# A sliding-window copy with two DMA queues: other staging groups, ten staged batches instead of eleven, 16 KB direct packets

## The chip, the cores and the metric

The kernel runs on one core of a Trainium2 chip. The metric is the device time of one execution in microseconds (us). No compute engine takes part: everything is done by the core's 16 DMA engines, fed by two queues, the direct one (issued by the SyncE engine, SP; q1 in the profile) and the staging one (issued by ScalarE, ACT; q10).

Runs went to several chips of one kind. The kernel before took 757 us on the first and 750 to 752 us on the others, so I compare kernels by their ratio to the kernel before on the same chip. A ratio is the mean time of one kernel's fast runs over that of the other's of the same rounds; it is not quite the ratio of the medians that I quote.

## The reference

```python
batch, length, dim = (32, 4096, 256)      # float32, window_size 64, stride 32
n_windows = (length - window_size) // stride + 1          # 127
for i in range(n_windows):
    start = i * stride
    result[:, i] = x[:, start:start + window_size].copy()
```

In blocks of 32 rows (32 KB) a batch is 128 blocks, and window w is blocks w and w+1. Nearly every block is written twice, as the second (odd) half of one window and the first (even) half of the next.

## The kernel before

A batch is copied in one of two ways. **Direct**: HBM to HBM, each window read as 64 KB; one batch moves 8.3 MB through the DMA engines, and HBM both reads and writes it, 16.6 MB. **Staged**: its 4.2 MB are loaded once into an SBUF tile of 128 partitions and stored twice, as even and as odd halves; 12.6 MB through the engines, 12.6 MB in HBM. Staging so trades engine time for HBM traffic. Eleven batches are staged.

```python
DIRECT, IN, OUT = 32768, 16384, 16384      # largest packets, bytes
# ... class Copier: windows(), load(), store() issue one DMA each
class Staging:                              # 4 tiles of 128 x 32 KB
    def run(self, q):
        bufs = len(self.tiles)
        for g in range(min(bufs, len(self.batches))):
            self.load(q, g)                 # one DMA of 4 MB
        for g in range(len(self.batches)):
            self.store(q, g)                # two DMAs: even halves, odd halves
            if g >= 1 and g - 1 + bufs < len(self.batches):
                self.load(q, g - 1 + bufs)
# ... in the kernel:
staged = [*range(1, B - 3, 3), B - 2]       # 11 batches
spilled = staged[:-1]   # these store all 128 rows; the two rows too many land in
                        # neighbours' windows and are overwritten later by rest()
# ... direct batches, in transfers of 16 windows:
for j in range(7):
    if j % 3 == 1 or (j == 3 and i % 5 != 2):
        c.windows(ring_d, b, w0 + 16 * j, 16, 0)     # split into halves: two transfers
        c.windows(ring_d, b, w0 + 16 * j, 16, 1)
    else:
        c.windows(ring_d, b, w0 + 16 * j, 16)
# ... rest(b): 15 windows, after the neighbours' stores have landed
```

Of the kernel before, what the change touches and what calls it, by code (L numbers as in the profile page):

```python
# [1 line left out]

# [4 lines left out]


DIRECT, IN, OUT = 32768, 16384, 16384


class Copier:


    def __init__(self, nc, tc, x, out, B, L, D, W, S, n_win):
        assert W == 2 * S and L % S == 0
        self.nc, self.tc, self.x, self.out = nc, tc, x, out
        self.B = B
        self.blk = S * D
        self.nb = L // S  # L20
        self.nw = n_win
        self.total = 0
        self.done = tc.alloc_semaphore("done")

    def xap(self, block, dims):
        return bass.AP(self.x.tensor, self.x.offset + block * self.blk, dims)

    def oap(self, elem, dims):
        return bass.AP(self.out.tensor, self.out.offset + elem, dims)

    def count(self, dma):
        dma.then_inc(self.done, 16)
        self.total += 16

    def windows(self, q, b, w0, n, half=None):

        blk = self.blk
        size = 2 * blk if half is None else blk
        off = blk if half else 0
        self.count(  # L40
            q.dma_start(
                out=self.oap((b * self.nw + w0) * 2 * blk + off, [[2 * blk, n], [1, size]]),
                in_=bass.AP(
                    self.x.tensor,
                    self.x.offset + (b * self.nb + w0) * blk + off,
                    [[blk, n], [1, size]],
                ),
                max_dma_last_dim=DIRECT,
            )
        )  # L50

    def load(self, q, t, b):
        return q.dma_start(
            out=t[:, :], in_=self.xap(b * self.nb, [[self.blk, self.nb], [1, self.blk]]),
            max_dma_last_dim=IN,
        )

    def store(self, q, t, b, half, p0=0, n=None):



        blk = self.blk
        n = self.nb if n is None else n
        w = b * self.nw + p0 - half
        return q.dma_start(
            out=self.oap(w * 2 * blk + half * blk, [[2 * blk, n], [1, blk]]),
            in_=t[p0 : p0 + n, :],
            max_dma_last_dim=OUT,
        )


class Staging:


    def __init__(self, c, pool, dtype, batches, bufs):
        self.c, self.batches = c, batches
        self.tiles = [pool.tile([128, c.blk], dtype, name=f"xb{i}") for i in range(bufs)]
        self.loaded = [c.tc.alloc_semaphore(f"loaded{i}") for i in range(bufs)]
        self.stored = [c.tc.alloc_semaphore(f"stored{i}") for i in range(bufs)]

    def load(self, q, g):
        n, i = divmod(g, len(self.tiles))
        if n:
            q.wait_ge(self.stored[i], 32 * n)
        self.c.load(q, self.tiles[i], self.batches[g]).then_inc(self.loaded[i], 16)

    def store(self, q, g):
        n, i = divmod(g, len(self.tiles))
        q.wait_ge(self.loaded[i], 16 * (n + 1))
        if g == len(self.batches) - 1:  # L90

            for half, p0, rows in ((0, 0, 112), (0, 112, 15), (1, 1, 15), (1, 16, 112)):
                self.c.count(self.c.store(q, self.tiles[i], self.batches[g], half, p0, rows))
            return
        for half in (0, 1):
            self.c.store(q, self.tiles[i], self.batches[g], half).then_inc(self.stored[i], 16)

    def wait_stored(self, q, g):
        n, i = divmod(g, len(self.tiles))
        q.wait_ge(self.stored[i], 32 * (n + 1))  # L100

    def run(self, q):
        bufs = len(self.tiles)
        for g in range(min(bufs, len(self.batches))):
            self.load(q, g)
        for g in range(len(self.batches)):
            self.store(q, g)

            if g >= 1 and g - 1 + bufs < len(self.batches):
                self.load(q, g - 1 + bufs)  # L110


@with_exitstack
def kernel(
    ctx: ExitStack,
    tc: tile.TileContext,
    x: bass.AP,
    window_size: bass.AP,
    stride: bass.AP,
    out: bass.AP,  # L120
):
    nc = tc.nc
    W, S = int(window_size), int(stride)
    B, L, D = x.shape
    n_win = (L - W) // S + 1
    assert out.shape == (B, n_win, W, D)
    c = Copier(nc, tc, x, out, B, L, D, W, S, n_win)
    staged = [*range(1, B - 3, 3), B - 2]
    direct = [b for b in range(B) if b not in staged]
    pool = ctx.enter_context(tc.tile_pool(name="xb", bufs=1))  # L130
    st = Staging(c, pool, x.dtype, staged, 4)
    ring_d, ring_s = nc.sync, nc.scalar
    spilled = staged[:-1]

    def rest(b):

        for n in (b - 1, b + 1):
            if n in spilled:
                st.wait_stored(ring_d, spilled.index(n))
        c.windows(ring_d, b, 0 if b - 1 in spilled else 112, 15)  # L140

    with tc.tile_critical():
        st.run(ring_s)



        free = [b for b in direct if b - 1 not in spilled and b + 1 not in spilled]
        direct = free + [b for b in direct if b not in free]
        late = 4
        for i, b in enumerate(direct):  # L150
            w0 = 15 if b - 1 in spilled else 0
            for j in range(7):
                if j % 3 == 1 or (j == 3 and i % 5 != 2):
                    c.windows(ring_d, b, w0 + 16 * j, 16, 0)
                    c.windows(ring_d, b, w0 + 16 * j, 16, 1)
                else:
                    c.windows(ring_d, b, w0 + 16 * j, 16)
            if b in free:
                rest(b)
            elif i >= len(free) + late:  # L160
                rest(direct[i - late])
        for b in direct[-late:]:
            rest(b)
        ring_d.wait_ge(c.done, c.total)


# [1 line left out]
_INS = ['x', 'window_size', 'stride']  # L168
_OUTS = [((32, 127, 64, 256), 'float32')]

_NUMBERS = {'window_size': 64, 'stride': 32}


# [26 lines left out]
```

## Time and profile before

| | kernel before |
|---|---|
| time | 756.73 us median, 4 runs |
| bytes through the DMA engines | 313.2 MB |
| HBM read + written | 220.9 + 267.0 = 487.9 MB |

The page of the kernel before, its parts on time slices and queues. The DMA line gives the busy tenths of the 16 engines in 40 slices of 19 us, the GB/s line what they moved; a queue's line gives packets, MB, and the time its packets took as a share of 16 engines' span.

```profile
DMA  9999999999999999999999999999999999999996
GB/s 372 429 400 423 409 431 426 420 420 408 408 435 418 408 413 430 408 413 434 431 403 418 425 411 408 425 426 402 416 422 428 393 428 423 419 425 422 415 398 294
DMA packets 17949, 313.16 MB, mean 414 GB/s; under 512 B 4169, under 2 KB 4169, under 8 KB 4169
...
q1 hardware_dynamic: 8945, 174.80, 55.2%
q10 hardware_dynamic: 9002, 138.35, 44.1%
...
HBM read 220.92 MB, written 266.99 MB: 644 GB/s over the span
```

The engines are always busy, yet between the first slice and the last the rate swings between 393 and 435 GB/s. A packet that waits for HBM counts as busy. The records of single packets show it. Undisturbed, a 16 KB packet takes 611 ns, a 32 KB packet 1213 ns and a semaphore write 9 ns, each overlapping the next by 3 to 4 ns; longer times are time lost. I call the sum of such excess, averaged over the 16 engines, the *contention*: 22.9 us here.

The DMA view of two stretches of the same run, chosen from the packet records, first one in which the staging queue only stores (204 to 222 us), then one at the change from stores to loads (240 to 252 us). A queue's line has packets, MB and share as above:

```profile
q1 hardware_dynamic: 222, 4.16, 53.8%
q10 hardware_dynamic: 223, 3.59, 46.5%
```

```profile
q1 hardware_dynamic: 138, 2.72, 57.5%
q10 hardware_dynamic: 137, 1.98, 41.0%
```

Two readings. The queues take turns packet by packet (222 against 223, 138 against 137), as the Trainium skill's page "DMA: Bandwidth & Descriptors" (Queues, rings and completion order) says; semaphore writes count as turns. And direct bytes weigh twice in HBM: the first stretch, 18 us long, drew (2 x 4.16 + 3.59) MB / 18 us = 662 GB/s and moved 431 GB/s, no packet lengthened to speak of; the second, 12 us long, drew 618 GB/s and moved 392, its packets 8% over their undisturbed times. Two more stretches of stores (undisturbed) and one more change (8%) look the same.

SP's own waits (total us, times, longest):

```profile
SPq L41 <- DMA out_dram<-xb: 100.2, 6, 42.7
```

These cost nothing as long as the direct queue still holds work, which the slices of the whole page show: they stay at 9 tenths.

### The profile page before, as it was taken

What the parts mean: (1) busy time and instruction counts of PE and PEld (TensorE: products, weight loads), DVE (VectorE), ACT (ScalarE), POOL (GpSimd) and SP (SyncE); (2) the same over time, 40 slices, a digit from 0 to 9 for tenths busy, and PEclk for the clock granted to TensorE, in tenths of its full rate; (3) what the DMA queues carried; (4) which work ended last, traced back from release to release, by engine and by line L of the source; (5) the groups of instructions that cost most, each with busy time, mean ns of one, the idle gap of its engine ahead of it and who ended that gap; (6) DMA issues with size and microseconds to landing.
All of it is one profiled execution on the core that took longest, in us unless ns stands there. A gap on an engine that the chain in (4) does not pass through costs nothing. (4 is left out here: it accounts for less than half of the span.)

```text
span 757.3 us, 312 instructions
## 1 busy us (share of the span) xinstructions
POOL 0.2 (0%) x4
## 2 busy tenths in 40 slices
POOL 0000000000000000000000000000000000000000
DMA  9999999999999999999999999999999999999996
GB/s 372 429 400 423 409 431 426 420 420 408 408 435 418 408 413 430 408 413 434 431 403 418 425 411 408 425 426 402 416 422 428 393 428 423 419 425 422 415 398 294
DMA packets 17949, 313.16 MB, mean 414 GB/s; under 512 B 4169, under 2 KB 4169, under 8 KB 4169
## 3 DMA queue, kind: packets, MB, share of 16 engines
q1 hardware_dynamic: 8945, 174.80, 55.2%
q10 hardware_dynamic: 9002, 138.35, 44.1%
q14 instruction: 2, 0.02, 0.0%
HBM read 220.92 MB, written 266.99 MB: 644 GB/s over the span
## 5 line engine op out<-in xcount | busy, mean ns | idle before, releaser
L181 POOL MEMSET const-bfloat16-1.0<- 128x1 bf16 x1 | 0.1, 102 | 0.0
L181 POOL MEMSET const-uint8-127<- 128x1 uint8 x1 | 0.1, 102 | 0.0
L181 POOL MEMSET const-float32-0.0<- 128x1 f32 x1 | 0.1, 99 | 0.2 <-issue 0.2
L181 POOL MEMSET const-float32-1.0<- 128x1 f32 x1 | 0.1, 99 | 0.0
## 6 DMA issues: line engine op xcount, KB each, us to landing
out_dram<-in_x_dram SPq DMA_DIRECT2D x88, 1024.0 KB, 95.2
out_dram<-xb ACTq DMA_DIRECT2D x20, 4096.0 KB, 115.1
out_dram<-in_x_dram SPq DMA_DIRECT2D x118, 512.0 KB, 94.4
xb<-in_x_dram ACTq DMA_DIRECT2D x11, 4096.0 KB, 90.0
out_dram<-in_x_dram SPq DMA_DIRECT2D x21, 960.0 KB, 95.0
out_dram<-xb ACTq DMA_DIRECT2D x2, 3584.0 KB, 93.4
out_dram<-xb ACTq DMA_DIRECT2D x2, 480.0 KB, 94.9
```

The costliest lines, as they stand in the source:

```text
L181: nc = _bacc.Bacc("TRN2", target_bir_lowering=False, num_devices=1)
```

## The change

It simplifies the kernel. Staging works in groups of 16 blocks, one for each DMA engine, in slots whose 16 partitions lie on 16 different SBUF ports; loads and stores alternate finely, one load and then two stores, with loads ten groups ahead. Ten batches are staged. Direct batches go out as one transfer of 112 windows in 16 KB packets and one of 15 windows in 32 KB packets. No store spills, so SP waits for none. The partitions follow the port map of the skill's page "SBUF — State Buffer" (Door 1: The DMA port swizzle). The diff is shortened; `# ...` marks what is left out.

```diff
-DIRECT, IN, OUT = 32768, 16384, 16384
+DIRECT, STAGE = 16384, 16384
+N_STAGED = 10
+N_TILES = 6
+LEAD = 10
+# class Direct
+        full = self.g.nw // 16 * 16
+        for b in self.batches:
+            self.windows(q, b, 0, full, DIRECT)
+            self.windows(q, b, full, self.g.nw - full, 2 * DIRECT)
+# class Staged
+        self.slots = [t[32 + c : 96 : 4, :] for t in tiles for c in range(4)]
+        self.groups = [(b, j) for b in batches for j in range(0, g.nb, 16)]
+    # ... load(): one DMA of 16 blocks into a slot
+    # ... store(): two DMAs, even and odd halves; 15 rows at a batch's edges
+    def run(self, q, lead):
+        for r in range(lead):
+            self.load(q, r)
+        for r in range(len(self.groups)):
+            if r + lead < len(self.groups):
+                self.load(q, r + lead)
+            self.store(q, r)
-    staged = [*range(1, B - 3, 3), B - 2]
-    # ... rest(), the split window transfers, 4 tiles of 128 partitions
+    staged = Staged(g, tc, pool, x.dtype, range(B - N_STAGED, B), N_TILES)
+    direct = Direct(g, range(B - N_STAGED))
```

More of the change, by code (lines that the diff above doesn't have):

```diff
@@ L6, with __init__, xap, oap @@
 from concourse._compat import with_exitstack
-DIRECT, IN, OUT = 32768, 16384, 16384
-class Copier:
-    def __init__(self, nc, tc, x, out, B, L, D, W, S, n_win):
-        assert W == 2 * S and L % S == 0
-        self.nc, self.tc, self.x, self.out = nc, tc, x, out
-        self.B = B
-        self.blk = S * D
-        self.nb = L // S
-        self.nw = n_win
-        self.total = 0
-        self.done = tc.alloc_semaphore("done")
-    def xap(self, block, dims):
-        return bass.AP(self.x.tensor, self.x.offset + block * self.blk, dims)
-    def oap(self, elem, dims):
-        return bass.AP(self.out.tensor, self.out.offset + elem, dims)
+DIRECT, STAGE = 16384, 16384
+N_STAGED = 10
+N_TILES = 6
+LEAD = 10
+class Geometry:
+    def __init__(self, tc, x, out, B, L, D, W, S, n_win):
+        assert W == 2 * S and L % S == 0 and n_win == L // S - 1
+        self.x, self.out = x, out
+        self.blk, self.nb, self.nw = S * D, L // S, n_win
+        self.done, self.total = tc.alloc_semaphore("done"), 0
+    def xap(self, b, block, dims):
+        return bass.AP(self.x.tensor, self.x.offset + (b * self.nb + block) * self.blk, dims)
+    def oap(self, b, w, half, dims):
+        at = ((b * self.nw + w) * 2 + half) * self.blk
+        return bass.AP(self.out.tensor, self.out.offset + at, dims)
     def count(self, dma):
@@ L33, in count @@
         self.total += 16
-    def windows(self, q, b, w0, n, half=None):
-        blk = self.blk
-        size = 2 * blk if half is None else blk
-        off = blk if half else 0
-        self.count(
-            q.dma_start(
-                out=self.oap((b * self.nw + w0) * 2 * blk + off, [[2 * blk, n], [1, size]]),
-                in_=bass.AP(
-                    self.x.tensor,
-                    self.x.offset + (b * self.nb + w0) * blk + off,
-                    [[blk, n], [1, size]],
-                ),
-                max_dma_last_dim=DIRECT,
-            )
-        )
@@ L52, in load @@
-    def load(self, q, t, b):
-        return q.dma_start(
-            out=t[:, :], in_=self.xap(b * self.nb, [[self.blk, self.nb], [1, self.blk]]),
-            max_dma_last_dim=IN,
-        )
-    def store(self, q, t, b, half, p0=0, n=None):
-        blk = self.blk
-        n = self.nb if n is None else n
-        w = b * self.nw + p0 - half
-        return q.dma_start(
-            out=self.oap(w * 2 * blk + half * blk, [[2 * blk, n], [1, blk]]),
-            in_=t[p0 : p0 + n, :],
-            max_dma_last_dim=OUT,
-        )
@@ L72, with __init__, windows, run @@
-class Staging:
-    def __init__(self, c, pool, dtype, batches, bufs):
-        self.c, self.batches = c, batches
-        self.tiles = [pool.tile([128, c.blk], dtype, name=f"xb{i}") for i in range(bufs)]
-        self.loaded = [c.tc.alloc_semaphore(f"loaded{i}") for i in range(bufs)]
-        self.stored = [c.tc.alloc_semaphore(f"stored{i}") for i in range(bufs)]
-    def load(self, q, g):
-        n, i = divmod(g, len(self.tiles))
+class Direct:
+    def __init__(self, g, batches):
+        self.g, self.batches = g, batches
+    def windows(self, q, b, w0, n, size):
+        g = self.g
+        g.count(
+            q.dma_start(
+                out=g.oap(b, w0, 0, [[2 * g.blk, n], [1, 2 * g.blk]]),
+                in_=g.xap(b, w0, [[g.blk, n], [1, 2 * g.blk]]),
+                max_dma_last_dim=size,
+            )
+        )
+    def run(self, q):
+        full = self.g.nw // 16 * 16
+        for b in self.batches:
+            self.windows(q, b, 0, full, DIRECT)
+            self.windows(q, b, full, self.g.nw - full, 2 * DIRECT)
@@ new lines, with __init__, load @@
+class Staged:
+    def __init__(self, g, tc, pool, dtype, batches, n_tiles):
+        self.g = g
+        tiles = [pool.tile([128, g.blk], dtype, name=f"xb{i}") for i in range(n_tiles)]
+        self.slots = [t[32 + c : 96 : 4, :] for t in tiles for c in range(4)]
+        self.loaded = [tc.alloc_semaphore(f"loaded{i}") for i in range(len(self.slots))]
+        self.stored = [tc.alloc_semaphore(f"stored{i}") for i in range(len(self.slots))]
+        self.groups = [(b, j) for b in batches for j in range(0, g.nb, 16)]
+    def load(self, q, r):
+        g, (b, j) = self.g, self.groups[r]
+        n, i = divmod(r, len(self.slots))
@@ L83, in load, with store @@
         if n:
             q.wait_ge(self.stored[i], 32 * n)
-        self.c.load(q, self.tiles[i], self.batches[g]).then_inc(self.loaded[i], 16)
-    def store(self, q, g):
-        n, i = divmod(g, len(self.tiles))
+        q.dma_start(
+            out=self.slots[i], in_=g.xap(b, j, [[g.blk, 16], [1, g.blk]]),
+            max_dma_last_dim=STAGE,
+        ).then_inc(self.loaded[i], 16)
+    def store(self, q, r):
+        g, (b, j) = self.g, self.groups[r]
+        n, i = divmod(r, len(self.slots))
@@ L89, in store @@
         q.wait_ge(self.loaded[i], 16 * (n + 1))
-        if g == len(self.batches) - 1:
-            for half, p0, rows in ((0, 0, 112), (0, 112, 15), (1, 1, 15), (1, 16, 112)):
-                self.c.count(self.c.store(q, self.tiles[i], self.batches[g], half, p0, rows))
-            return
         for half in (0, 1):
-            self.c.store(q, self.tiles[i], self.batches[g], half).then_inc(self.stored[i], 16)
-    def wait_stored(self, q, g):
-        n, i = divmod(g, len(self.tiles))
-        q.wait_ge(self.stored[i], 32 * (n + 1))
@@ L102, in run @@
-    def run(self, q):
-        bufs = len(self.tiles)
-        for g in range(min(bufs, len(self.batches))):
-            self.load(q, g)
-        for g in range(len(self.batches)):
-            self.store(q, g)
-            if g >= 1 and g - 1 + bufs < len(self.batches):
-                self.load(q, g - 1 + bufs)
+            lo = 1 if half and j == 0 else 0
+            hi = 15 if not half and j + 16 == g.nb else 16
+            dma = q.dma_start(
+                out=g.oap(b, j + lo - half, half, [[2 * g.blk, hi - lo], [1, g.blk]]),
+                in_=self.slots[i][lo:hi, :],
+                max_dma_last_dim=STAGE,
+            )
@@ L113 @@
+            if r + len(self.slots) < len(self.groups):
+                dma.then_inc(self.stored[i], 16)
+            else:
+                g.count(dma)
+    def run(self, q, lead):
[5 more added lines that the diff above has]
+            self.store(q, r)
 @with_exitstack
@@ L126 @@
     assert out.shape == (B, n_win, W, D)
-    c = Copier(nc, tc, x, out, B, L, D, W, S, n_win)
-    staged = [*range(1, B - 3, 3), B - 2]
-    direct = [b for b in range(B) if b not in staged]
+    g = Geometry(tc, x, out, B, L, D, W, S, n_win)
     pool = ctx.enter_context(tc.tile_pool(name="xb", bufs=1))
-    st = Staging(c, pool, x.dtype, staged, 4)
-    ring_d, ring_s = nc.sync, nc.scalar
-    spilled = staged[:-1]
-    def rest(b):
-        for n in (b - 1, b + 1):
-            if n in spilled:
-                st.wait_stored(ring_d, spilled.index(n))
-        c.windows(ring_d, b, 0 if b - 1 in spilled else 112, 15)
-    with tc.tile_critical():
-        st.run(ring_s)
-        free = [b for b in direct if b - 1 not in spilled and b + 1 not in spilled]
-        direct = free + [b for b in direct if b not in free]
-        late = 4
-        for i, b in enumerate(direct):
-            w0 = 15 if b - 1 in spilled else 0
-            for j in range(7):
-                if j % 3 == 1 or (j == 3 and i % 5 != 2):
-                    c.windows(ring_d, b, w0 + 16 * j, 16, 0)
-                    c.windows(ring_d, b, w0 + 16 * j, 16, 1)
-                else:
-                    c.windows(ring_d, b, w0 + 16 * j, 16)
-            if b in free:
-                rest(b)
-            elif i >= len(free) + late:
-                rest(direct[i - late])
-        for b in direct[-late:]:
-            rest(b)
-        ring_d.wait_ge(c.done, c.total)
+    staged = Staged(g, tc, pool, x.dtype, range(B - N_STAGED, B), N_TILES)
+    direct = Direct(g, range(B - N_STAGED))
+    with tc.tile_critical():
+        staged.run(nc.scalar, LEAD)
+        direct.run(nc.sync)
+        nc.sync.wait_ge(g.done, g.total)
 _INS = ['x', 'window_size', 'stride']
```

## The prediction

> **What bounds it.** The page's second part shows the 16 DMA engines busy in every slice but the last (9 tenths; mean 414 GB/s); no compute engine works. The engines are the limit. The trace's packet records show how: on one engine, packets of the two queues alternate strictly, one from each, and follow each other without a gap. A 32 KB packet takes 1213 ns undisturbed, a 16 KB one 611 ns, a semaphore write 9 ns, each overlapping the next by 3 to 4 ns; so a packet costs about 5 ns plus its bytes at 27.2 GB/s. The Trainium skill's page "DMA: Bandwidth & Descriptors" (Queues, rings and completion order) says that an engine takes turns between its queues packet by packet; this trace agrees, semaphore writes counting as turns.
>
> Sum for one of the 15 fuller engines, before: direct 21 x 8 windows x 2 packets x 1209.5 = 406.4 us; staged 11 x 24 blocks x 2 packets x 607.5 = 320.8; semaphores 1.5; together 728.7. Start and end take 3.6. The span is 757.3, so about 25 us (3.4%) are packets that took longer than their undisturbed time. Mean packets say the same: 1248 and 632 ns. I take this for contention in HBM (644 GB/s over the span, page part 3). It is uneven: nearly none while the staged queue stores even halves, about 40 ns lost per us while it loads, bursts of over 100 ns per us at changes from one to the other.
>
> **What the change does.**
> - One direct batch more, one staged fewer, no spilled stores: 313.2 MB moved falls to 308.3 MB. HBM traffic rises from 487.9 to 491.4 MB.
> - Direct packets become 16 KB (windows 112 to 126 stay 32 KB), 5 ns each.
> - Per fuller engine: direct 22 x (28 x 607.5 + 2 x 1209.5) = 427.4 us; staged 10 x 24 x 2 x 607.5 = 291.6; semaphores 1.6; together 720.6. That is 8 us less, all on the critical path.
> - Turns per engine are about 704 (direct) against 720 (staged), so both queues end together as before.
> - The 15-row transfers should leave one engine with about 10% less, as before (the same page's rule: the largest count up to 16 that divides the rows).
> - Waits: the loads run ten groups ahead and 24 slots exist, so the staged queue should never run dry; 240 staging issues at about 0.4 us (ACT's DMA issues, timeline) are hidden. Waits of SP for stores (100 us, SP's waits) vanish, but they cost nothing: the queue was full.
> - Loads and stores are mixed finely at all times, instead of in 4 MB runs. Neighbouring engines now touch neighbouring blocks. This changes the contention, whose sign I cannot read from the trace: the weighted mean of its load and store stretches gives 25 ns per us (18 us), the mixed stretches over 60 (45 us); HBM would have to give 2% more per us.
>
> **Prediction.** 720.6 + 3.6 + about 22 us of contention = 746 us, range 733 to 768. Faster by over 2%: 0.33; within 2%: 0.58; slower by over 2%: 0.09.
>
> **What would show each step.** Moved bytes 308 MB, HBM reads 225 MB and writes 266 MB; undisturbed packets still 611 and 1213 ns; DMA 9 tenths to the last slice; the two queues ending within about 10 us; mean 16 KB packet 625 to 632 ns.
>
> **What would make it wrong.** The contention: if fine mixing removes it, about 727 us; if every stretch behaves like the mixed ones of before, 770 or more. Less likely: a queue that runs dry (slices under 9 tenths), or a split of the 16-row transfers over fewer than 16 engines or ports, which would show in longer undisturbed packets.

## The result, and the profile after

The changed kernel took 766.75 us (median of 4 runs, 765.12 to 769.9) against 756.73 us; ratio 1.0137, 95% interval 1.0113 to 1.0161. It is slower, by an amount inside the 2% band.

Its page, the same parts:

```profile
DMA  8999999999999999999999999999999999999995
GB/s 358 397 412 410 413 411 407 413 410 412 409 407 413 410 414 410 405 414 409 398 410 413 403 414 406 411 412 409 410 405 407 414 412 408 410 406 410 404 405 222
DMA packets 22660, 308.32 MB, mean 403 GB/s; under 512 B 4502, under 2 KB 4502, under 8 KB 4502
...
q1 hardware_dynamic: 11198, 183.11, 58.6%
q10 hardware_dynamic: 11460, 125.19, 40.1%
...
HBM read 225.05 MB, written 266.34 MB: 642 GB/s over the span
```

The bytes are those predicted. The rate is now flat, near 410, without the slices of 430. Total HBM rate is as good as before, 642 against 644 GB/s.

The DMA view from 100 to 300 us, first of the kernel before, then of the changed one:

```profile
DMA packets 4823, 83.83 MB, mean 419 GB/s; under 512 B 1130, under 2 KB 1130, under 8 KB 1130
...
q1 hardware_dynamic: 2410, 46.67, 56.0%
q10 hardware_dynamic: 2412, 37.16, 44.4%
```

```profile
DMA packets 6015, 82.06 MB, mean 410 GB/s; under 512 B 1185, under 2 KB 1185, under 8 KB 1185
...
q1 hardware_dynamic: 3008, 49.23, 60.4%
q10 hardware_dynamic: 3006, 32.82, 40.3%
```

With direct bytes counted twice, HBM moved (2 x 46.67 + 37.16) / 200 us = 652 GB/s before and (2 x 49.23 + 32.82) / 200 us = 656 GB/s after. The rate at the engines fell and the rate at HBM did not: this is what a ceiling on HBM traffic would look like.

Where the 7.6 us of the two profiled spans (757.3 and 764.9) came from, out of the packet records. I followed each engine by joining packets whose start meets another's end, and averaged the 15 fuller engines; the sixteenth has less work and ends early. The first packet's time counts from the start of the span.

| us | before | after | difference |
|---|---|---|---|
| undisturbed packets | 727.9 | 720.4 | -7.5 |
| contention | 22.6 | 34.0 | +11.4 |
| last engine behind the mean | 3.1 | 6.4 | +3.3 |
| first packet | 2.0 | 2.4 | +0.4 |

They sum to +7.6; from the last packet to the end of the span it is 1.7 us in both. SP's waits for stores in mid-run are gone, as planned; what is left is its wait for the end:

```profile
SPq L127 <- DMA out_dram<-xb: 83.5, 1, 83.5
```

### The profile page after: what moved, and what is told of

It is laid out like the page before. It is cut to its first block, busy times and chain, and to the rows that moved or that the text cites. A ratio compares the mean times of both kernels' runs of the same rounds, so it can differ in the third digit from the quotient of the medians.

```text
span 764.9 us, 334 instructions
## 1 busy us (share of the span) xinstructions
POOL 0.2 (0%) x4
```

## The experiments

Each run below gave correct results, except the one that was made wrong. "Contention" is again the mean excess of packets over their undisturbed times, from that run's packet records.

### Three parts of the change undone singly

**e1_phases**, loads and stores in coarse runs again:

```diff
-            if r + lead < len(self.groups):
-                self.load(q, r + lead)
-            self.store(q, r)
+        # ... first the loads of two batches; n = 8 groups; then, for each batch b:
+            for half in (0, 1):
+                for r in range(b * n, (b + 1) * n):
+                    self.store(q, r, half)
+            if b + 2 < batches:
+                for r in range((b + 2) * n, (b + 3) * n):
+                    self.load(q, r)
```

> The changed kernel with its staging queue in coarse order: eight loads of a batch, then its eight even-half stores, then its eight odd-half stores, as the kernel before had it; groups, ports, packets and the direct queue unchanged, so bytes and turns are equal. Theory M (loads mixed finely among stores cause the extra contention): the time falls by at least 10 us, to 745 to 755 us, and mean 16 KB packets fall from 640 to about 630 ns. Rival P (direct packets of 16 KB in 112-row transfers) and rival A (neighbouring engines now work on neighbouring blocks): the time stays at 760 to 770 us.

Measured: 761.62 us, ratio 1.0151 (1.0134 to 1.0168), contention 26.3 us.

**e2_halves**, direct copies as 16 window halves in 32 KB packets:

```diff
-            self.windows(q, b, 0, full, DIRECT)
-            self.windows(q, b, full, self.g.nw - full, 2 * DIRECT)
+            for w0 in range(0, self.g.nw, 16):
+                for half in (0, 1):
+                    self.windows(q, b, w0, min(16, self.g.nw - w0), half)   # 32 KB packets
```

> The changed kernel with its direct copies cut as 16 window halves per transfer, packets of 32 KB, so that the same bytes take the same 704 turns of an engine (352 packets and 352 semaphore writes). Rival P expects 745 to 755 us. Theories M and A expect 760 to 770 us (the per-packet cost of 5 ns saves nothing here, a semaphore write costs as much).

Measured: 760.57 us, ratio 1.0125 (1.0088 to 1.0161), contention 23.1 us.

**e3_pitch**, the rows of a group 8 blocks apart:

```diff
-in_=g.xap(b, j, [[g.blk, 16], [1, g.blk]]),
+in_=g.xap(b, j, [[8 * g.blk, 16], [1, g.blk]]),
-out=g.oap(b, j + lo - half, half, [[2 * g.blk, hi - lo], [1, g.blk]]),
+out=g.oap(b, j + 8 * lo - half, half, [[16 * g.blk, hi - lo], [1, g.blk]]),
 # ... groups and the 15-row edge renumbered to match
```

> The changed kernel with the rows of a staged group 8 blocks apart (256 KB in the input) instead of adjacent; same transfers, bytes and turns. Rival A expects 745 to 755 us, or at least a change of over 5 us in either direction; theories M and P expect 762 to 771 us, no change.

Measured: 758.88 us, ratio 1.0113 (1.0097 to 1.0128), contention 27.5 us.

None brings the time back to the kernel before (750.64 us on this chip). This chip had no control run of the changed kernel, so differences of half a per cent among the three say little, and the bands above, which I took from the first chip's 766 us, do not fit it (e3 fell into none of them). The changed kernel, measured later on two chips of like speed, has ratios of 1.006 and 1.008; the three are at 1.011 to 1.015, so no part undone made it faster. My first theory, that fine mixing of loads among stores is what hurts, found no support.

### Loads without HBM

**e4_sbuf_load**, wrong: after the first 20 groups the loads copy out of one fixed SBUF slot (20 slots are left for the groups instead of 24).

```diff
-out=self.slots[i], in_=g.xap(b, j, [[g.blk, 16], [1, g.blk]]),
+out=self.slots[i], in_=self.fixed if r >= 20 else g.xap(b, j, [[g.blk, 16], [1, g.blk]]),
```

> The changed kernel, all but its first 20 group loads (and one fixed load) replaced by copies of the same shape out of one fixed SBUF slot: the same bytes through engines and SBUF write ports, but no HBM read for them; the result is wrong on purpose. If the loads' reads of HBM are what lengthens packets, mean 16 KB packets fall below 620 ns outside of the start and the time falls to 730 to 740 us. If it is their writes to SBUF or the mere presence of a third kind of transfer, the time stays at 760 to 770 us.

Measured: 736.61 us (one run; the kernel before 750.64 us), contention 5.3 us, nearly all of it in the first 150 us, while loads still read HBM. The DMA view of 300 to 500 us:

```profile
DMA packets 6325, 86.17 MB, mean 431 GB/s; under 512 B 1250, under 2 KB 1250, under 8 KB 1250
...
q1 hardware_dynamic: 3163, 51.66, 60.2%
q10 hardware_dynamic: 3162, 34.51, 40.5%
```

The engines run at 431 GB/s, close to the 435 GB/s of the skill's page "DMA: Bandwidth & Descriptors" (Where 436 GB/s comes from), with the same transfers, packets and turns. A third of the staged bytes no longer touch HBM, which is left with (2 x 51.66 + 2/3 x 34.51) / 200 us = 632 GB/s. So the contention goes away with the loads' HBM reads; the loads' writes to SBUF and the number of kinds of transfer, which stayed, cause none of it.

That led to theory H: HBM gives one core about 655 to 665 GB/s of mixed traffic and no more. At the engines' full pace the changed kernel asks for more: 60.0% of the bytes from 100 to 300 us are direct (49.23 of 82.06 MB), 431 GB/s x 1.600 = 690.

### The ceiling by itself, and the number of staged batches

**c_after** is the changed kernel as it is.

> The changed kernel as it is, as the control of this chip. Theory H (the chip's HBM, not the DMA engines, sets the pace while loads run) and its rivals expect the earlier ratio to the kernel before, 1.011 to 1.017.

Measured: 755.73 us, ratio 1.0059 (1.0044 to 1.0074), contention 23.7 us. That is below the band I expected. The loss depends on the chip: here the middle of the run (100 to 300 us) draws 666 GB/s from HBM, on the first chip 656:

```profile
q1 hardware_dynamic: 3054, 49.96, 60.5%
q10 hardware_dynamic: 3050, 33.30, 40.2%
```

**all_direct** stages nothing:

```diff
-    staged = Staged(g, tc, pool, x.dtype, range(B - N_STAGED, B), N_TILES)
-    direct = Direct(g, range(B - N_STAGED))
+    direct = Direct(g, range(B))
-        staged.run(nc.scalar, LEAD)
```

> All 32 batches direct, nothing staged: 266.3 MB through the engines, 532.7 MB in HBM. Theory H: HBM cannot give more than the 650 to 665 GB/s that the changed kernel drew in its middle, so about 800 to 825 us, with packets a quarter or more over their undisturbed time. Rival S (only the staged loads disturb; direct copies alone run undisturbed): 32 x 19.43 us of packets, 625 to 640 us.

Measured: 810.5 us (one run). Its page, then the DMA view of 300 to 500 us:

```profile
q1 hardware_dynamic: 16288, 266.34, 98.3%
HBM read 266.34 MB, written 266.34 MB: 659 GB/s over the span
```

```profile
q1 hardware_dynamic: 4072, 66.59, 99.6%
```

The engines are 98% busy at 329 GB/s, three quarters of what they can move. HBM's rate in the middle, 2 x 66.59 MB / 200 us = 666 GB/s, is the same as with ten staged batches. The rival, 625 to 640 us, is out.

**n11** and **n12** stage 11 and 12 batches in the changed kernel's way. To keep the two queues' turns equal, direct copies go out in transfers of 16 windows instead of 112, some of them split into halves in n12; so more than the number of batches differs from the changed kernel.

```diff
-N_STAGED = 10
+N_STAGED = 11        # n12: 12
-            self.windows(q, b, 0, full, DIRECT)
+            # ... 16 KB packets (in n11 the last 15 windows in 32 KB)
+            for i, w0 in enumerate(range(0, g.nw, 16)):
+                # i in SPLIT (n12: 1, 3, 5): two transfers of window halves; else one
```

> The changed kernel with 11 staged batches instead of 10 (as many as the kernel before), and direct copies cut in transfers of 16 windows so that both queues have about 795 turns. Engine time per fuller engine rises by 9.7 us, HBM traffic falls by 4.2 MB to 487.3 MB. Theory H: 4.2 MB at 655 GB/s, 6 us less than the changed kernel, ratio to the kernel before 1.000 to 1.008. Rival E (the engines' own sum of packets sets the pace and the added contention is a constant share): 10 us more than the changed kernel, ratio 1.022 to 1.030.

> The same with 12 staged batches (864 and 860 turns). Theory H: another 6 us less as long as HBM sets the pace; the engines' sum, 738.5 us and about 4 for start and end, is then close below, so 8 to 13 us less than the changed kernel, ratio 0.995 to 1.004. Rival E: 20 us more than the changed kernel, ratio about 1.04.

Measured: n11 750.11 us, ratio 0.9986 (0.9967 to 1.0006), contention 8.4 us; n12 757.66 us, ratio 1.0087 (1.0070 to 1.0104), contention 5.4 us. The stretch from 100 to 300 us of c_after, n11 and n12, in that order, has its rate in the last column:

```profile
100.00:300.00 200.00, 0.00 (x0) 1.00 1.01 416
```

```profile
100.00:300.00 200.00, 0.00 (x0) 1.00 1.01 426
```

```profile
100.00:300.00 200.00, 0.00 (x0) 1.00 1.01 428
```

The queues in that stretch, of n11 and then of n12:

```profile
q1 hardware_dynamic: 3451, 47.60, 56.2%
q10 hardware_dynamic: 3449, 37.66, 44.6%
```

```profile
q1 hardware_dynamic: 3701, 45.16, 53.1%
q10 hardware_dynamic: 3705, 40.49, 47.7%
```

With the direct shares of those stretches (0.600, 0.558, 0.527) this is 666, 664 and 654 GB/s in HBM. A test that uses no rate of these three runs: at the 431 GB/s of e4 they would ask HBM for 690, 671 and 658 GB/s, which against the 666 of all_direct on the same chip is 3.6% too much, 0.8% too much and none. Their packets in that stretch took 3.5%, 0.9% and 0.4% over their undisturbed times. The first two stand at the ceiling. The third has come off it: the engines are the limit, their sum of packets is 10 us longer than n11's, and the time rises by 7.6 us. I had expected n12 still to gain: that missed, because n11 had already won back all but 8 us of contention and there was little left to win.

### Both kernels' forms with ten batches

**c_after_b** is the control again.

> The changed kernel as it is, again as a control, because its ratio to the kernel before differed between two chips (1.014 and 1.006) and the first three experiments had no control on their chip. Theory H: between 1.004 and 1.016, the higher the slower this chip's HBM is.

Measured: 756.36 us, ratio 1.0076 (1.0061 to 1.0091), contention 24.2 us.

**e123_all** has the three edits of e1, e2 and e3 together.

> The changed kernel with the edits of the first three experiments together (coarse order of staging, direct copies as 16 window halves of 32 KB, staged rows 8 blocks apart), still 10 staged batches. Theory H: within 0.6% of this chip's control, since HBM traffic is the same. Rival F (the form of the transfers, through any of the three or their sum, causes the loss): at least 8 us under the control, at or below the kernel before.

Measured: 764.88 us, ratio 1.0184 (1.0154 to 1.0214), contention 26.8 us. It missed H's band and went away from what rival F expected: undoing the forms together costs 1.1% against the control, though bytes are equal, so H's ceiling alone does not set the time. About 2.6 us of that are contention; most of the rest is a last engine that ends 12 us behind the mean, 6.4 in the control. Why the engines drift apart so far I did not find out.

**b10** is the kernel before with batch 30 direct, and its direct transfers no longer split into halves:

```diff
-    staged = [*range(1, B - 3, 3), B - 2]
+    staged = [*range(1, B - 3, 3)]
-                if j % 3 == 1 or (j == 3 and i % 5 != 2):
+                if False:
```

> The kernel before with one change: batch 30 is copied directly instead of staged, so 10 staged batches; window halves are no longer split, which keeps the queues' turns near each other (528 and 510). HBM traffic rises by 4.1 MB. Theory H: 5 to 9 us slower than the kernel before, ratio 1.006 to 1.013, near the control. Rival F: not slower, 0.990 to 1.002, since the engines' sum is 9.7 us smaller.

Measured: 751.39 us, ratio 1.0009 (0.9993 to 1.0025), contention 23.9 us. H's number missed. I had counted only the added HBM traffic and forgotten that the kernel before is limited by the engines in its store stretches: one staged batch fewer makes the packets' undisturbed sum 9.9 us shorter (713.9 against 723.8 us, mean of 16 engines), and the contention grows by 11 us against the same kernel with eleven batches (c_before below, on another chip of like speed). The trade is even. So on such chips the number of staged batches alone does not make the changed kernel slower, and what sets it 5 us behind b10 is in its form. Contention is the same in both. The last engine trails the mean by 6.4 us in the control and 3.5 us in b10, and by count of packets a fuller engine's undisturbed sum is 2.1 us longer in the control (720.6 against 718.5 us: smaller direct packets, more semaphore writes); the two make up most of the 5 us.

**n11_tail** spreads the last 15 windows of a direct batch over 16 engines, with 32 KB packets elsewhere (diff against n11):

```diff
+        part = 2 * g.blk // 16
+        dims = lambda step: [[part, 16], [step, n], [1, part]]     # 4 KB pieces
```

> A version meant to beat both: the changed kernel with 11 staged batches, direct copies in transfers of 16 windows with 32 KB packets, and the last 15 windows of a direct batch spread over 16 engines in 4 KB pieces instead of 15 engines. Engine sum per fuller engine 404.6 + 320.8 + 2 = 727 us, 3 less than the version with 11 before, and no engine ends early through the direct copies. Theory H and this sum expect a ratio of 0.990 to 0.997; if 4 KB packets are dear or the balance does not matter, 0.998 to 1.005.

Measured: 768.02 us, ratio 1.0233 (1.0216 to 1.0249), a clear miss. Its 4 KB packets are not dear (159 ns for most, which is 27.2 GB/s and the usual few ns). Yet its mean contention was 27 us with the bytes of n11. A reading of it, argued and not shown by this run: while the tail's small packets take turns with 16 KB staged packets, HBM has little to do; while whole windows in 32 KB packets do, it is asked for too much. That suggested that evenness counts beside the total.

### Evenness

With what was still open, I ran four more on another chip. **c_before** is the kernel before.

> The kernel before, for a profile on the chip of the next runs. Theory H: on a chip where it takes about 751 us, its packets lose about 15 to 18 us per engine to contention (23 us on the first chip, where it took 757), more than the 8 us of the even version with 11 staged batches and less than the 24 us of the changed kernel on such chips.

Measured: 749.25 us (one run), contention 13.1 us, a little less than expected. On like chips the changed kernel loses 24 us: again 11 us more, as on the first chip, where the time before was 757.

**n11_b** repeats n11.

> The even version with 11 staged batches again, as the control of this chip: ratio to the kernel before 0.996 to 1.001.

Measured: 751.29 us, ratio 1.0006 (0.9989 to 1.0023), contention 10.3 us.

**n11_uneven** has the same bytes, with large direct steps first and small ones later (diff against n11):

```diff
-                packet = DIRECT if n == 16 else TAIL
-                if i in SPLIT:
+                packet = 32768 if b < 10 else 16384
+                if b >= 10:
```

> The same 11 staged batches and the same bytes, but the direct queue takes large steps first and small ones later: batches 0 to 9 as whole windows in 32 KB packets (24 turns a batch), batches 10 to 20 as window halves in 16 KB packets (48 turns), 768 turns in all against 792. At the engines' pace HBM would have to give 722 GB/s in the first part and about 640 in the second. Evenness theory: some 25 us lost in the first part, nothing in the second, 12 to 25 us slower than the control. If only totals count: within 4 us of the control.

Measured: 767.3 us, ratio 1.0223 (1.0197 to 1.0249), 16 us over its control, contention 26.0 us. The DMA view of 100 to 300 us and then of 450 to 650 us:

```profile
q1 hardware_dynamic: 2434, 53.04, 68.0%
q10 hardware_dynamic: 2433, 26.61, 32.3%
```

```profile
DMA packets 7823, 85.45 MB, mean 427 GB/s; under 512 B 2607, under 2 KB 2607, under 8 KB 2607
...
q10 hardware_dynamic: 3923, 42.85, 50.5%
q1 hardware_dynamic: 3898, 42.59, 50.3%
```

In the first stretch HBM gives (2 x 53.04 + 26.61) / 200 us = 663 GB/s, the ceiling again, and the engines move only 398. In the second they ask for (2 x 42.59 + 42.85) / 200 us = 640 GB/s and run nearly free at 427. What HBM could have given in the second part does not make up for the first. That it is not the 32 KB packets as such, the next run shows, with 12 us of contention.

**n11_32k** has 32 KB packets in both queues (diff against n11):

```diff
-DIRECT, TAIL, STAGE = 16384, 32768, 16384
+DIRECT, TAIL, STAGE = 32768, 32768, 32768      # and SPLIT = (3,)
```

> The even version with 32 KB packets in both queues (525 and 528 turns): half as many packets at about 5 ns each, 2.8 us less for an engine, with the same mix of direct and staged bytes. Expected 2 to 4 us under the control, ratio to the kernel before 0.992 to 0.997; if coarser packets make contention worse, at or over the control.

Measured: 752.81 us, ratio 1.0028 (1.0013 to 1.0043), contention 12.0 us. It did not beat its control beyond noise: in the two profiled runs 3 us fewer in packets met 1.7 us more contention, and the span was 1.2 us shorter, but the medians differ by 1.5 us the other way. No version of mine beat the kernel before beyond noise; n11 equals it and beats the changed kernel by 0.7% on the same chip.

## Why the prediction was wrong

- *Bytes and undisturbed packets.* Right. 308.3 MB, HBM 225 and 266 MB; a fuller engine's packets were forecast at 728.7 and 720.6 us and came to 727.9 and 720.4.
- *Queues, waits, slots.* Right. The direct queue ended at 757.0 us and the staging queue at 763.1; slices between the first and the last stayed at 9 tenths; SP's removed waits gave nothing back.
- *"About 22 us of contention."* This term failed, and with it the sign. I had named it as the one that could make the sum wrong. It was 34 us on the first chip, 11 more than before, where I had taken 3 off; the mean 16 KB packet took 640 ns, not 625 to 632. I read contention as a matter of neighbouring transfers, averaged its rate over load and store stretches, and so kept it constant. The runs show a ceiling on the rate of HBM reads plus writes in its place: 656 GB/s on the first chip, about 660 to 667 on the others, the same for direct shares from 0.56 to 1. Above it, contention is demand over ceiling, as c_after, n11 and all_direct show on one chip; on the first chip it is 690 / 656, or 5.2%, and the changed kernel's packets took 5.0% over their undisturbed times (these two are nearly one measurement, since 656 is that kernel's own rate). Whether the limit lies in HBM or on the way to it, and whether other addresses would move it, no run tells. Nor is it one number for every moment: on the first chip stretches of stores alone drew up to 668 GB/s undisturbed, and changes from stores to loads lost 8% at 618 to 624. I had noted that "HBM would have to give 2% more per us" and did not price it.
- *"All on the critical path."* Half true. 7.5 us less engine time is worth 7.5 us only where the engines set the pace; in b10, 9.9 us less bought nothing. The changed kernel stands at the ceiling nearly all its run.
- *The start and the end, 3.6 us.* The last engine's lag behind the mean was not a term of its own; in the kernel before it hid in the 25 us that I took for contention (22.6 and 3.1 in the table). It grew by 3.3 us. The mean engine had no idle time to speak of (2.4 + 720.4 + 34.0 = 756.8 us is where it ended), and packets per engine are equal on 15 engines, so the lag too should be lengthened packets, shared unequally. What shares them so stays open; I made no run that isolates it.

With what was measured the sum is 720.4 + 34.0 + 6.4 + 2.4 + 1.7 = 764.9 us, the profiled span. That the time still lies between the 733 and 768 us that I gave is owed to the width of that range and not to the mechanism.

Shown: the ceiling (all_direct, n11_uneven), that the loads' HBM reads use up the room (e4), that one more staged batch takes most contention away in the changed kernel's form (n11) and one fewer adds 11 us in the other (b10). Not shown: why the engines end further apart in the changed kernel than in b10; what the port layout, group size or missing spills add is not told apart by these runs.

## What to carry to other kernels

When DMA engines are 100% busy, divide bytes by time at both ends of the transfer; if lengthened packets come with a constant HBM rate, HBM sets the pace, and fewer bytes at the engines buy nothing if they add bytes in HBM. With two limits close together, the best mix is where both are just met, and it must hold at every moment, since packet sizes and semaphore writes decide how two queues share the engines. Compare on the same chip: the same change cost 1.4% on one chip and 0.6 to 0.8% on two others.

## What the Trainium skill lacked or had wrong

- "HBM Reference" (Specifications) gives about 716 GB/s for a domain, and the text below its table has a core streaming alone bounded by its DMA engines at about 425 GB/s. Copies from HBM to HBM by one core stopped at 659 GB/s of reads plus writes (329 GB/s at the engines, all_direct), so a limit other than the engines can bound a single core. The page has no figure for mixed reads and writes.
- The same page does not say that chips differ: the changed kernel's middle drew 656 GB/s on one chip and 666 and 667 on two others.
- No page says that the mix matters. On the first chip, stretches of stores beside direct copies ran undisturbed at 662 GB/s, while one at the change from stores to loads got 618, with lengthened packets.
- "DMA: Bandwidth & Descriptors" (Queues, rings and completion order) has an engine drain a whole packet, typically about 9 to 17 descriptors, from one queue before it turns to the other. Here a turn was a single record of 16 or 32 KB, or a single semaphore write: 3008 against 3006 turns in 200 us. If such a record is one descriptor, as its size suggests, the typical figure does not hold for this case.
